# A chunked SSM scan by pairs of chunks, in a two-block transformer kernel

## Chip, cores and metric

The kernel runs on one core of one Trainium2 chip. The metric is the device time of one execution in microseconds (us); the time stated for a kernel is the median of its runs.

## What is computed

Two transformer blocks on 512 tokens of width 1024. The first mixes gated linear attention (GLA, four heads) with a grouped complex-diagonal state-space model (SSM) and ends in a feed-forward layer; the second has latent attention, a convolution and a mixture of experts. The change lies in the SSM of the first block. Its core in the reference:

```python
def step(carry, u_blk):
    h_re, h_im = carry
    bu_re = jnp.einsum('bcgh,gnh->bcgn', uf, bb_re)
    bu_im = jnp.einsum('bcgh,gnh->bcgn', uf, bb_im)
    acc_re, acc_im, x_re, x_im = lax.associative_scan(
        _complex_combine, (lam_b_re, lam_b_im, bu_re, bu_im), axis=1)
    s_re = x_re + acc_re * h_re[:, None] - acc_im * h_im[:, None]
    s_im = x_im + acc_re * h_im[:, None] + acc_im * h_re[:, None]
    y = jnp.einsum('bcgn,ghn->bcgh', s_re, cr) - jnp.einsum('bcgn,ghn->bcgh', s_im, ci)
    return (s_re[:, -1], s_im[:, -1]), y
```

That is x_t = L x_(t-1) + B u_t with a complex diagonal L, y_t = Re(C x_t) + D u_t, for 64 groups of 16 channels with 64 states each, and a gelu behind it. All is in float32; large products are made of three passes with operands split into a high and a low part.

## The kernel before

The 528 tokens (16 learned ones in front) are cut into 66 chunks of 8 (`NCH`). The SSM is computed in eighths of its groups (`ei`, 8 of them):

- `ssm_states` (L282): for each eighth a table G of the powers of L times B is formed, one half on DVE (L295 to L297), one on POOL (L299 to L301); PE transposes it (L307), ACT copies it out (L308), PE multiplies it with the inputs U (L314), and ACT writes each chunk's own contribution into the tile H (L317), which holds 66 chunks x real and imaginary x 32 columns.
- `ssm_scan` (L328): on POOL, for the chunks 1 to 64 one after the other, H[c] += L^8 H[c-1], as a 128x128 product (L334) and two 128x64 sums (L335, L336). `sct` is its buffer, in turn one of two.
- `ssm_out` (L407), a generator of steps: for each eighth `ssm_prep` (the tables CL on DVE, L352 to L354, a strip for short distances, stored to `k_dram`), `ssm_load` (U by POOL's queue, Tb by SP's and POOL's) and `ssm_main` (L380): ACT copies states from H into HS (L387), PE adds up L393 (Tb with U) and L396 (CL with HS), ACT makes the gelu ys (L399) and stores it to `gs_dram`.

Around it run the four heads of GLA: `gla_proj` (projections, PE's bulk work) and `gla_chain` (the recurrence). Generators are woven: `weave(main, fill)` takes a step of `fill` behind each step of `main`. The states and the scan are traced in the projections of heads 0 and 1; two steps of `outs` (the generator `ssm_out`) around head 2; and in head 3 `both(lagged(2), outs)` takes `outs` along from the fifth of six steps on (`LATE` = 4). What is left of it runs beside the last chain and `z_gate` (gate projections, eight units each for two gates, `zth`, stored to `gate_dram`). Then come `mix_gla` (L724; it loads o by L734 and splits it into ohi and olo), `load_gs` (L750; it loads `gs_dram` back and PE transposes it, L759) and `mix_ssm`.

Each engine works through its own queue in order. The order in a queue is made by a scheduler from the order of tracing and a simulated timeline; waits follow from the tiles that are read and written. Weights come by SP's queue (`raw`, L65), ACT casts the high part (`whi`, L73), DVE subtracts the low one (`wlo`, L74), one block ahead of its use (`Weights`); `raw` has two buffers.

Of the kernel before, what the change touches and what calls it, by code (L numbers as in the profile page):

```python
# [11 lines left out]
F32 = mybir.dt.float32  # L12
# [4 lines left out]
OP = mybir.AluOpType  # L17
# [6 lines left out]
NTOK = NMETA + SEQ  # L24
NCH = NTOK // 8
# [3 lines left out]
SPREAD = 14  # L29
BACK = 14  # L30
RATE = 2.0
LATE = 4
NS = 4
FIRST = 1
EARLY14 = 2
# [107 lines left out]
def sincos_exp(e, sp, mid, keep):  # L143

    nc, tc, A = e.nc, e.tc, e.A
    V = nc.vector
# [90 lines left out]
    V.tensor_scalar(lam[:, 0, 1], pw[:, 1, 8], -1.0, None, op0=OP.mult)  # L237
    V.tensor_copy(lam[:, 1, 0], pw[:, 1, 8])
    V.tensor_copy(lam[:, 1, 1], pw[:, 0, 8])
    zr, zi = T("x"), pw[:, 1, 1]  # L240
    V.tensor_scalar(zr, pw[:, 0, 1], -1.0, None, op0=OP.add)
    den, w = T("k"), T("p")
# [39 lines left out]
def ssm_states(e, sp):  # L282
# [3 lines left out]
    for ei in range(8):  # L286
# [23 lines left out]
        for ri in range(2):  # L310
            p = e.ps()
            for g2 in range(2):
                for q in range(4):
                    nc.tensor.matmul(p[64 * g2:64 * g2 + 64, q * NCH:(q + 1) * NCH],  # L314
                                     lhsT=GT[:, ri, q, 64 * g2:64 * g2 + 64], rhs=U[:, g2, q, :],
                                     start=True, stop=True)
            nc.scalar.copy(e.H[:, :, ri, q0:q0 + 4].rearrange("p c q -> p q c"),  # L317
                           p[:, :4 * NCH].rearrange("p (q c) -> p q c", q=4))


def load_u(e, sp, q0, bufs):
# [6 lines left out]
def ssm_scan(e, sp):  # L328
    nc = e.nc
    g = nc.gpsimd  # L330
    H = e.H
    for c in range(1, NCH - 1):
        t = e.sct[c % 2]
        g.tensor_mul(t, H[:, c - 1:c].to_broadcast([128, 2, 2, 32]), e.lam)  # L334
        g.tensor_add(H[:, c], H[:, c], t[:, :, 0])  # L335
        g.tensor_add(H[:, c], H[:, c], t[:, :, 1])  # L336


def ssm_prep(e, sp, ei):

    nc, A = e.nc, e.A
    V = nc.vector
    g0 = 8 * ei
    cr = sp.tile([128, 2, 8, 16], F32, name="craw", bufs=2)
    nc.gpsimd.dma_start(cr, A["ssm_c"][:, :, g0:g0 + 8, :])
    dsk = sp.tile([128, 2, 16], F32, name="dsk", bufs=2)
    nc.gpsimd.dma_start(dsk, A["d_diag"][:, ei])
    CL = sp.tile([128, 8, 9, 16], F32, name="CL", bufs=2)
    t = sp.tile([128, 8, 9, 16], F32, name="CLt", bufs=1)
    power = lambda i: e.pws[:, i, :, g0:g0 + 8].rearrange("p k g -> p g k")[:, :, :, None].to_broadcast([128, 8, 9, 16])  # L350
    coeff = lambda i: cr[:, i][:, :, None, :].to_broadcast([128, 8, 9, 16])
    V.tensor_mul(CL, power(0), coeff(0))  # L352
    V.tensor_mul(t, power(1), coeff(1))
    V.tensor_sub(CL, CL, t)  # L354
    p = e.ps()
    for s in range(2):
        for j in range(4):
            g = 4 * s + j
            nc.tensor.matmul(p[32 * j:32 * j + 32, s * 128:(s + 1) * 128],
                             lhsT=e.bs[:, g0 + g:g0 + g + 2].rearrange("p g h -> p (g h)"),  # L360
                             rhs=CL[:, g, 0:8].rearrange("p k h -> p (k h)"), start=True, stop=True)
    stt = sp.tile([128, 2, 128], F32, name="strip", bufs=1)
    nc.scalar.copy(stt.rearrange("p s n -> p (s n)"), p[:, :256])
    V.tensor_add(stt[:, :, 0:16], stt[:, :, 0:16], dsk)
    nc.gpsimd.dma_start(e.k_dram[g0:g0 + 8, :, 112:240].rearrange("(s j) h n -> (j h) s n", j=4), stt)
    return CL


def ssm_load(e, sp, ei):
    nc = e.nc  # L370
    U = load_u(e, sp, 4 * ei, 1)
    T = sp.tile([128, 8, 128], F32, name="Tb", bufs=1)
    kd = e.k_dram[8 * ei:8 * ei + 8, 0:16]
    for k in range(8):
        (nc.gpsimd if k % 2 else nc.sync).dma_start(T[16 * k:16 * k + 16],
# [4 lines left out]
def ssm_main(e, sp, ei, CL, U, T):  # L380
    nc = e.nc
    q0 = 4 * ei
    HS = sp.tile([128, 4, 2, 64], F32, name="HS", bufs=1)
    with behind(e, (e.k_last,)):
        for g2 in range(2):
            for ri in range(2):
# [337 lines left out]
def mix_gla(e, pool, ws):  # L724
# [3 lines left out]
    ohi = e.mb.tile([128, 8, 512], F32R, name="ohi", tag="u", bufs=3)  # L728
    olo = e.mb.tile([128, 8, 512], F32R, name="olo", tag="u", bufs=3)
    e.mixed = e.mb.tile([128, 8, 512], F32, name="mixed", tag="u", bufs=3)  # L730
    o = pool.tile([128, 8, 512], F32, name="o")
    for h in range(4):
        r = o[:, 2 * h:2 * h + 2]
        nc.sync.dma_start(r, e.o_dram[:, 2 * h:2 * h + 2])  # L734
        nc.scalar.copy(ohi[:, 2 * h:2 * h + 2], r)
        V.tensor_sub(olo[:, 2 * h:2 * h + 2], r, ohi[:, 2 * h:2 * h + 2].bitcast(F32))
# [1207 lines left out]
def block(ctx, tc, A, out, stop=None, dbg=None):  # L1944
# [78 lines left out]
    s_keep = ExitStack()  # L2023
    keep = s_keep.enter_context(P(name="ssmk", bufs=1, **R))
    e.H = keep.tile([128, NCH, 2, 32], F32, name="H")
    e.sct = [keep.tile([128, 2, 2, 32], F32, name=f"sct{i}") for i in range(2)]
    s1 = ExitStack()
    sp = s1.enter_context(P(name="ssm1", bufs=1, **R))
    wa, wgu = gate_weights(e, sp)
# [5 lines left out]
    s2 = ExitStack()  # L2035
    bpp = s2.enter_context(P(name="bp", bufs=1, **Lf))
    bp = bpp.tile([128, 4, NTOK], F32, name="bp")
    e.seg = bpp.tile([128, NTOK], F32, name="seg")
    nc.gpsimd.memset(e.seg, 1.0)
    for s0 in (0, 16, 144, 272, 400):  # L2040
        nc.gpsimd.memset(e.seg[:, s0:s0 + 1], 0.0)
    gp = s2.enter_context(P(name="gla", bufs=1, **Lf))
    e.Sb = [gp.tile([128, 4, 128], F32, name=f"Sb{i}") for i in range(2)]
    for t in e.Sb:
# [3 lines left out]
    for i in range(2):  # L2048
        last = nc.gpsimd.tensor_copy(e.xm[:, :, i * NMETA:(i + 1) * NMETA], e.xn[i][:, :, :NMETA])
    with P(name="gt", bufs=1, **R) as gtp:  # L2050
        kz = gtp.tile([128, 112], F32, name="kz")
        with tc.issue_after(last.ins):
            nc.gpsimd.memset(kz, 0.0)
# [27 lines left out]
                next(b, None)  # L2081
            yield

    def both(a, b):
        for i, _ in enumerate(a):
            if i >= LATE:
                next(b, None)
            yield
        for _ in b:
            yield  # L2090

    rest = scanned()
    weave(gla_proj(e, gp, 1, ws, parts[1]), twice(lagged(0), rest))
    for _ in rest:
# [5 lines left out]
    next(outs)  # L2100
    weave(gla_proj(e, gp, 2, ws, parts[2]), lagged(1))
    next(outs)
    weave(gla_proj(e, gp, 3, ws, parts[3]), both(lagged(2), outs))
    s_mb = ctx.enter_context(ExitStack())
    s4 = ExitStack()
    zz = s4.enter_context(P(name="zz", bufs=1, **R))
# [416 lines left out]
```

## Time and profile before

| | us |
|---|---|
| median of three runs | 1525.13 (1523.4 to 1525.76) |
| profiled execution, its own time | 1523.06 |
| its span, first to last instruction | 1521.2 |
| PE busy (matmul) | 1440.6 |
| PE weight load busy | 1198.0 |
| DVE busy | 882.6 |
| ACT busy | 655.8 |
| POOL busy | 510.7 |

PE is TensorE, DVE VectorE, ACT ScalarE, POOL GpSimd, SP SyncE; a q behind an engine's name is its queue of DMA issues. Busy times of the engines overlap. The granted clock is TensorE's share of full speed in a stretch: 1.00 is 2.4 GHz, 0.50 is 1.2 GHz.

### The profile page before, as it was taken

To read this page: it belongs to the slowest core of one execution; us is meant where nothing else is said; L and a number is where in the kernel's file an instruction comes from. 1 tells how busy PE (TensorE), PEld (TensorE's weight loads), DVE (VectorE), ACT (ScalarE), POOL (GpSimd) and SP (SyncE) were. 2 spreads that over 40 slices of the span, in tenths; PEclk is the share of its full clock that TensorE was granted. 3 is DMA by queue.
4 is the path that set the end of the run, shared out by engine and by line. 5 is a ranking of instruction groups with operands and counts; after the bars stand their busy time and mean duration, and the time that the engine had idled before them with its cause. 6 is when DMAs were issued, how large, how long until landed. Compare 5 with 4: busy or idle time off the path is not lost. (4 is left out here: it accounts for less than half of the span.)

```text
span 1521.2 us, 22633 instructions
## 1 busy us (share of the span) xinstructions
PE 1440.6 (95%) x8832; PEld 1198.0 (79%) x8832; DVE 882.6 (58%) x1539; ACT 655.8 (43%) x1081; POOL 510.7 (34%) x583
## 2 busy tenths in 40 slices
PE   7999999899999999999999999999999999978984
PEld 7989998677888899877787779987777877965542
DVE  6586644446245566645455454854798777544545
ACT  6464333545223343423313142547777673343323
POOL 0356888222001121412212121008877624012104
PEclk9999999999999999999999999999999999988997
DMA  5842232468553351655455444411222245868997
GB/s 211 189 93 99 86 93 101 107 170 253 169 209 111 127 206 36 214 180 176 143 194 180 153 165 139 151 59 55 96 75 72 90 153 215 347 246 313 413 407 166
DMA packets 73943, 253.42 MB, mean 167 GB/s; under 512 B 20912, under 2 KB 25792, under 8 KB 57188
## 3 DMA queue, kind: packets, MB, share of 16 engines
q1 hardware_dynamic: 38256, 180.18, 33.0%
q0 software_dynamic: 16192, 49.54, 11.7%
q10 hardware_dynamic: 19380, 22.17, 4.6%
q8 instruction: 72, 1.18, 0.3%
q14 instruction: 43, 0.35, 0.1%
HBM read 226.65 MB, written 32.17 MB: 170 GB/s over the span
## 5 line engine op out<-in xcount | busy, mean ns | idle before, releaser
L74 DVE TENSOR_TENSOR wlo<-raw,whi 128x2048 fp32r<-128x2048 f32 x73 | 177.7, 2434 | 125.5 <-ACT whi L73 125.5
L73 ACT CAST whi<-raw 128x2048 fp32r<-128x2048 f32 x76 | 145.2, 1910 | 195.3 <-PE ps L98 100.0
L1119 POOL TENSOR_TENSOR uc<-uc,u 128x512 f32<-128x512 f32 x77 | 114.7, 1490 | 92.5 <-ACT u L1116 86.0
L97 PE MATMUL ps<-xhi,whi 128*128 128x264 f32 (+1 forms) x352 | 119.0, 340 | 0.0
L98 PE MATMUL ps<-xlo,whi 128*128 128x264 f32 (+1 forms) x352 | 117.9, 335 | 0.3 <-DVE xlo L1932 0.3
L99 PE MATMUL ps<-xhi,wlo 128*128 128x264 f32 (+1 forms) x352 | 117.5, 334 | 0.0
L99 PE MATMUL ps<-hn,wlo 128*128 128x512 f32 (+1 forms) x256 | 97.7, 382 | 0.0
L98 PE MATMUL ps<-hn,whi 128*128 128x512 f32 (+1 forms) x256 | 97.6, 382 | 0.0
L97 PE MATMUL ps<-hn,whi 128*128 128x512 f32 (+1 forms) x256 | 97.5, 383 | 0.0
L866 DVE SCALAR_TENSOR_TENSOR aacc<-araw,ca,aacc 128x1024 f32<-128x1024 f32 x42 | 55.0, 1310 | 51.1 <-DMA araw<-in_ada_w_dram 50.8
L97 PE MATMUL ps<-whi,hh 128*128 128x512 f32 (+1 forms) x224 | 84.6, 378 | 0.0
L98 PE MATMUL ps<-wlo,hh 128*128 128x512 f32 (+1 forms) x224 | 84.1, 376 | 0.0
L99 PE MATMUL ps<-whi,hl 128*128 128x512 f32 (+1 forms) x224 | 83.9, 375 | 0.0
L905 POOL TENSOR_TENSOR fr<-fr 128x512 f32<-128x512 f32 x32 | 53.0, 1656 | 84.7 <-ACT fr L904 84.6
L862 POOL DMA_DIRECT2D araw<-in_ada_w_dram x48 | 26.3, 548 | 162.5 <-DVE aacc L866 94.5
L97 PE MATMUL ps<-whi,xhi 128*128 128x256 f32 x256 | 74.9, 292 | 0.0
L99 PE MATMUL ps<-whi,xlo 128*128 128x256 f32 x256 | 74.2, 290 | 0.0
L98 PE MATMUL ps<-wlo,xhi 128*128 128x256 f32 x256 | 73.5, 287 | 0.0
L97 PEld LDWEIGHTS ps<-xhi,whi 128*128 128x128 f32 x352 | 65.9, 188 | 8.9 <-issue 2.2
L99 PEld LDWEIGHTS ps<-xhi,wlo 128*128 128x128 f32 x352 | 66.3, 188 | 6.9
L98 PEld LDWEIGHTS ps<-xlo,whi 128*128 128x128 f32 x352 | 66.1, 188 | 6.8 <-DVE xlo L1932 0.5
L779 POOL TENSOR_TENSOR mixed<-mixed,mtb 128x512 f32<-128x512 f32 x8 | 12.5, 1559 | 152.7 <-DVE mtb L778 152.7
(673 smaller groups left out, 4162.4 us busy)
## 6 DMA issues: line engine op xcount, KB each, us to landing
raw<-in_w_ff_dram SPq DMA_DIRECT2D x28, 1024.0 KB
wg<-in_w_eg_dram SPq DMA_DIRECT2D x26, 1024.0 KB
araw<-in_ada_w_dram POOLq DMA_DIRECT2D x48, 512.0 KB
wd<-in_w_ed_dram SPq DMA_DIRECT2D x10, 1024.0 KB
raw<-in_w_glu_dram SPq DMA_DIRECT2D x8, 1024.0 KB
wse<-in_w_eg_dram SPq DMA_DIRECT2D x6, 1024.0 KB
y_dram<-wd SPq DMA_DIRECT2D x9, 512.0 KB
U<-u_dram POOLq DMA_DIRECT2D x16, 264.0 KB
```

The costliest lines, as they stand in the source:

```text
L73: nc.scalar.copy(hi[:, :n], raw[:, :n])
L74: sub.tensor_sub(lo[:, :n], raw[:, :n], hi[:, :n])
L97: nc.tensor.matmul(out, lhsT=ah, rhs=bh, start=(first and i == 0), stop=False)
L98: nc.tensor.matmul(out, lhsT=ah, rhs=bl, start=False, stop=False)
L99: nc.tensor.matmul(out, lhsT=al, rhs=bh, start=False, stop=(last and i == n - 1))
L779: nc.gpsimd.tensor_add(e.mixed[:, mm], e.mixed[:, mm], tb)
L862: nc.gpsimd.dma_start(raw, A["ada_w_2"][k * 128:(k + 1) * 128, i * DM:(i + 1) * DM])
L866: V.scalar_tensor_tensor(acc, raw, e.ca[:, k:k + 1], acc, op0=OP.mult, op1=OP.add)
L905: nc.gpsimd.tensor_mul(r, r, r)
L1119: nc.gpsimd.tensor_add(y, y, tmp)
```

## The change

Six edits go together.

1. The scan is made by pairs of chunks. `lam_step(e, 1, ..)`, six DVE instructions for an eighth (two products of 128x256 and four sums of 128x128), adds L^8 H[c-1] to all odd chunks of that eighth at once; it is traced one eighth behind the copies into H. `ssm_scan` then runs over the odd chunks only, 3 to 63, with the square of L^8 (`lam2`, six small DVE instructions in `sincos_exp`): 31 steps instead of 64. The even chunks are filled per eighth by `lam_step(e, 2, ..)`, ahead of the copies HS in `ssm_main`.
2. `sct` is one tile of 256 columns, used whole by `lam_step` and in halves by the scan.
3. CL is formed in two halves with half the buffer.
4. Tb gets two buffers.
5. The tile o in `mix_gla` becomes four tiles in three buffers; `seg`, the mask of the gates' scan, moves to another pool.
6. `both` is replaced by `second`, which takes a step of `outs` only behind the seventh step of `lagged(2)`; that generator has five, so none is taken in head 3.

```diff
@@ sincos_exp
+    lam2 = keep.tile([128, 2, 2, 32], F32, name="lam2", bufs=1)
+    V.tensor_mul(pt[:, 0], pw[:, 0, 8], pw[:, 0, 8])
+    V.tensor_mul(pt[:, 1], pw[:, 1, 8], pw[:, 1, 8])
+    V.tensor_sub(lam2[:, 0, 0], pt[:, 0], pt[:, 1])
+    V.tensor_copy(lam2[:, 1, 1], lam2[:, 0, 0])
+    V.scalar_tensor_tensor(lam2[:, 1, 0], pw[:, 0, 8], 2.0, pw[:, 1, 8], op0=OP.mult, op1=OP.mult)
+    V.tensor_scalar(lam2[:, 0, 1], lam2[:, 1, 0], -1.0, None, op0=OP.mult)
+    e.lam2 = lam2
@@ ssm_states, behind the copies into H
+        if ei:
+            lam_step(e, 1, q0 - 4)
+    lam_step(e, 1, 28)
+
+def lam_step(e, c0, q0):
+    V = e.nc.vector
+    q = slice(q0, q0 + 4)
+    t = e.sct.rearrange("p (c r q) -> p c r q", r=2, q=4)
+    for ro in range(2):
+        V.tensor_mul(t, e.H[:, c0 - 1:c0 + 63:2, :, q], e.lam[:, ro, :, q][:, None].to_broadcast([128, 32, 2, 4]))
+        for ri in range(2):
+            d = e.H[:, c0:c0 + 64:2, ro, q]
+            V.tensor_add(d, d, t[:, :, ri])
@@ ssm_scan
-    for c in range(1, NCH - 1):
-        t = e.sct[c % 2]
-        g.tensor_mul(t, H[:, c - 1:c].to_broadcast([128, 2, 2, 32]), e.lam)
+    for c in range(3, NCH - 2, 2):
+        t = e.sct[:, c % 4 // 2 * 128:c % 4 // 2 * 128 + 128].rearrange("p (o i q) -> p o i q", o=2, i=2)
+        g.tensor_mul(t, H[:, c - 2:c - 1].to_broadcast([128, 2, 2, 32]), e.lam2)
@@ ssm_prep
-    t = sp.tile([128, 8, 9, 16], F32, name="CLt", bufs=1)
-    V.tensor_mul(CL, power(0), coeff(0))
-    V.tensor_mul(t, power(1), coeff(1))
-    V.tensor_sub(CL, CL, t)
+    for g in (0, 4):
+        t = sp.tile([128, 4, 9, 16], F32, name="CLt", bufs=1)
+        V.tensor_mul(CL[:, g:g + 4], power(0, g), coeff(0, g))
+        V.tensor_mul(t, power(1, g), coeff(1, g))
+        V.tensor_sub(CL[:, g:g + 4], CL[:, g:g + 4], t)
@@ ssm_load
-    T = sp.tile([128, 8, 128], F32, name="Tb", bufs=1)
+    T = sp.tile([128, 8, 128], F32, name="Tb", bufs=2)
@@ ssm_main
+    lam_step(e, 2, q0)
@@ mix_gla
-    o = pool.tile([128, 8, 512], F32, name="o")
     for h in range(4):
-        r = o[:, 2 * h:2 * h + 2]
+        r = pool.tile([128, 2, 512], F32, name="o", bufs=3)
@@ block
-    e.sct = [keep.tile([128, 2, 2, 32], F32, name=f"sct{i}") for i in range(2)]
+    e.sct = keep.tile([128, 256], F32, name="sct")
-    e.seg = bpp.tile([128, NTOK], F32, name="seg")
+        e.seg = gtp.tile([128, NTOK], F32, name="seg")
-    def both(a, b):
-        for i, _ in enumerate(a):
-            if i >= LATE:
-                next(b, None)
-            yield
-        for _ in b:
-            yield
-    weave(gla_proj(e, gp, 3, ws, parts[3]), both(lagged(2), outs))
+    def second(a, b):
+        for i, _ in enumerate(a):
+            if i > 6:
+                next(b)
+            yield
+    weave(gla_proj(e, gp, 3, ws, parts[3]), second(lagged(2), outs))
```

## Rows read from the trace of the kernel before

**Rows 1.** Stretch 260 to 280: PE, PEld, DVE, ACT, POOL busy (count), clock, DMA, GB/s.

```profile
260.00:280.00 20.00, 13.16 (x88) 10.60 (x87) 6.01 (x9) 7.72 (x13) 10.69 (x26) 0.83 0.24 74
```

**Rows 2.** Waits between 264 and 280: total us, times, longest.

```profile
ACT HS L387 <- POOL H L336: 11.5, 1, 11.5
...
PE ps L396 <- ACT HS L387: 6.8, 2, 6.2
```

**Rows 3.** PE in order of time: start, us, instruction, [idle before <- releaser].

```profile
264.34 0.44 PE L393 MATMUL ps<-Tb,U 128*64 128x128 f32 x4
...
271.03 0.69 PE L396 MATMUL ps<-CL,HS 128*64 128x128 f32 x2 [6.25 <-ACT HS L387]
```

**Rows 4.** Stretch behind the idle time, columns as in rows 1.

```profile
271.00:276.50 5.50, 4.89 (x26) 3.33 (x28) 1.17 (x2) 3.63 (x6) 0.00 (x0) 0.51 0.02 3
```

**Rows 5.** Stretch of the later SSM outputs, columns as in rows 1.

```profile
280.00:400.00 120.00, 116.26 (x773) 91.18 (x773) 57.90 (x109) 58.56 (x89) 26.96 (x45) 1.00 0.69 194
```

**Rows 6.** POOL in order of time: the scan's first instruction and its last steps.

```profile
150.73 1.00 POOL L334 TENSOR_TENSOR sct<-H,lam 128x128 f32<-128x128 f32 x1
...
264.46 0.46 POOL L334 TENSOR_TENSOR sct<-H,lam 128x128 f32<-128x128 f32 x1
...
268.45 0.45 POOL L334 TENSOR_TENSOR sct<-H,lam 128x128 f32<-128x128 f32 x1
...
269.38 0.32 POOL L336 TENSOR_TENSOR H<-H,sct 128x64 f32<-128x64 f32 x1
```

**Rows 7.** DVE and POOL in order of time: single instructions.

```profile
43.82 0.28 DVE L225 TENSOR_TENSOR pw<-pw 128x128 f32<-128x128 f32 x1
...
105.53 1.51 DVE L633 TENSOR_TENSOR E<-E,k 128x256 f32<-128x256 f32 x1
...
244.24 2.35 DVE L74 TENSOR_TENSOR wlo<-raw,whi 128x2048 fp32r<-128x2048 f32 x1 [7.48 <-ACT whi L73]
...
244.52 2.39 POOL L334 TENSOR_TENSOR sct<-H,lam 128x128 f32<-128x128 f32 x1
...
250.80 0.43 DVE L633 TENSOR_TENSOR E<-E,k 128x256 f32<-128x256 f32 x1
```

**Rows 8.** Stretch of the states, columns as in rows 1.

```profile
98.00:150.00 52.00, 49.25 (x540) 45.73 (x539) 41.07 (x37) 26.68 (x44) 33.49 (x27) 1.00 0.29 96
```

**Rows 9.** That stretch: PE's wait, a DVE product, POOL's product by line.

```profile
PE ps L307 <- DVE G L297: 1.5, 3, 0.8
...
119.49 0.69 DVE L295 TENSOR_TENSOR G<-pw,bb 128x512 f32<-128x512 f32 x1 [0.48 <-PE ps L307]
...
L299 POOL TENSOR_TENSOR G<-pw,bb 128x512 f32<-128x512 f32 x6 | 10.2, 1696 | 1.5 <-PE ps L307 1.2
```

**Rows 10.** SP, ACT and PE in order of time, around outputs and o.

```profile
346.45 0.43 SPq L65 DMA_DIRECT2D raw<-in_w_zs_dram  x1
...
348.61 1.05 ACT L735 CAST ohi<-o 128x1024 fp32r<-128x1024 f32 x1 [4.17 <-DMA o<-o_dram]
...
379.02 0.64 ACT L387 COPY HS<-H 64x256 f32<-64x256 f32 x1
...
390.02 0.39 PE L396 MATMUL ps<-CL,HS 128*64 128x128 f32 x4
```

**Rows 11.** The end of the outputs: engines in order, DMA stretches, L759's instructions.

```profile
391.77 0.60 ACT L399 ACTIVATE ys<-ps 128x512 f32<-128x512 f32 x1 [1.31 <-PE ps L396]
...
396.50:397.00 0.50, 0.50 (x4) 0.41 (x3) 0.00 (x0) 0.00 (x0) 0.00 (x0) 1.00 0.00 0
...
399.26 2.29 DVE L74 TENSOR_TENSOR wlo<-raw,whi 128x2048 fp32r<-128x2048 f32 x1 [10.95 <-ACT whi L73]
...
401.58 0.32 SPq L65 DMA_DIRECT2D raw<-gs_dram  x1
...
404.00:404.50 0.50, 0.50 (x3) 0.40 (x3) 0.00 (x0) 0.00 (x0) 0.00 (x0) 1.00 0.23 90
...
L759 PE MATMUL ps<-ident,raw x32: 270/272/273, 413.9 to 455.7; 128*128 128x128 f32 x32
```

More of the change, by code (lines that the diff above doesn't have):

```diff
@@ L31 @@
 RATE = 2.0
-LATE = 4
 NS = 4
@@ L348, in ssm_prep @@
     CL = sp.tile([128, 8, 9, 16], F32, name="CL", bufs=2)
-    t = sp.tile([128, 8, 9, 16], F32, name="CLt", bufs=1)
-    power = lambda i: e.pws[:, i, :, g0:g0 + 8].rearrange("p k g -> p g k")[:, :, :, None].to_broadcast([128, 8, 9, 16])
-    coeff = lambda i: cr[:, i][:, :, None, :].to_broadcast([128, 8, 9, 16])
-    V.tensor_mul(CL, power(0), coeff(0))
-    V.tensor_mul(t, power(1), coeff(1))
-    V.tensor_sub(CL, CL, t)
+    power = lambda i, g: e.pws[:, i, :, g0 + g:g0 + g + 4].rearrange("p k g -> p g k")[:, :, :, None].to_broadcast([128, 4, 9, 16])
+    coeff = lambda i, g: cr[:, i, g:g + 4][:, :, None, :].to_broadcast([128, 4, 9, 16])
+    for g in (0, 4):
[3 more added lines that the diff above has]
+        V.tensor_sub(CL[:, g:g + 4], CL[:, g:g + 4], t)
     p = e.ps()
@@ L2037, in block @@
     bp = bpp.tile([128, 4, NTOK], F32, name="bp")
-    e.seg = bpp.tile([128, NTOK], F32, name="seg")
-    nc.gpsimd.memset(e.seg, 1.0)
-    for s0 in (0, 16, 144, 272, 400):
-        nc.gpsimd.memset(e.seg[:, s0:s0 + 1], 0.0)
     gp = s2.enter_context(P(name="gla", bufs=1, **Lf))
@@ L2050, in block @@
     with P(name="gt", bufs=1, **R) as gtp:
+        e.seg = gtp.tile([128, NTOK], F32, name="seg")
+        nc.gpsimd.memset(e.seg, 1.0)
+        for s0 in (0, 16, 144, 272, 400):
+            nc.gpsimd.memset(e.seg[:, s0:s0 + 1], 0.0)
         kz = gtp.tile([128, 112], F32, name="kz")
```

## Prediction

> **What bounds the kernel now.** I read the busy times first, then the table of stretches, then the waits, then the engines' lists around the one hole. PE is busy 1440.6 of 1521.2 us, so a change outside PE pays only where PE waits or runs at its low clock. Around the scan one stretch of 20 us stands out: from 260 to 280 us PE works only 13.16 us and its mean granted clock is 0.83 [rows 1]. The waits say why: ACT's copies HS (L387) waited 11.5 us for the last instruction of the scan on POOL (L336), and PE's L396 waited for HS, 6.8 us in two waits [rows 2]. In PE's own list the first four matmuls of the first SSM output (L393) start at 264.34, and L396 starts at 271.03 after 6.25 us of nothing [rows 3]; the other wait is the rest of the 6.8, 0.6 us. The granted clock tells the rest: after the hole PE gets 0.51, the lower level of 1.2 GHz, from 271.0 to 276.5, half of the 2.4 GHz that it has at 1.00 [rows 4]. So the scan ends too late for the place that the first SSM output has in PE's order. Elsewhere between 280 and 400 us PE is idle for only 3.7 of 120 us [rows 5].
>
> **What the change takes away: the hole.** The scan runs from 150.73 until 269.70 us: 64 steps, 1.86 us each on the average, 1.33 us where nothing disturbs one (268.45 - 264.46 is three steps) [rows 6]. The new one has 31 steps of the same three instructions, so 31 x 1.86 = 58 us, and ends near 153 + 58 = 211 us. Besides, the first output is traced later: with lagged(2) yielding five times, `i > 6` never comes, so the two steps of `outs` that lay in the last head are run by the loop behind it. The copies HS then stand at least one unit of z_gate and one step of chain 3 behind their old place. Either edit alone removes the wait: moved by two units of about 5.5 us (below), L396 would come at 264.8 + 11 = 276 us, and the old scan with the two copies for the first half would be through at 269.7 + 1.3 = 271. What is saved: 6.8 us of waiting, and half of the 4.89 us that PE worked at 0.51, 2.4 us [rows 2, 4]. Sum 9.2 us. Next late after it would be the small waits of the stretch from 280 to 400, 3.7 us in all [rows 5]; I leave them, with 3.7 us more gain as the lower bound: the second buffer of Tb may take some of them.
>
> **What it adds ahead of the scan.** lam_step(e, 1, ..) puts six DVE instructions behind each eighth: two of 128x256 and four of 128x128. The nearest rows: a 128x256 product took 0.43 us alone and 1.51 us beside POOL work, a 128x128 product 0.28 us [rows 7]. So one lam_step is 2 x 0.43 + 4 x 0.28 = 2.0 us undisturbed. I take the strides at nothing: a product of L295, which reads two broadcast views, took 0.69 us for 512 columns [rows 9], no more for an element than L633. Six of the eight lie between 98 and 150 us: 12 us more for DVE, which is busy 41.07 of 52 us there, so 10.9 are free [rows 8]. PE is idle for only 2.75 us there, but it does wait for DVE's G three times, 1.5 us in all [rows 8, 9]: G comes just in time. The free time lies after G, while DVE waits for PE to take G away (0.48 us ahead of that L295, released by L307 [rows 9]), and lam_step falls into it, traced an eighth back so that its H is long there. I take 3 us of new PE waiting, one half us for each of six. Bounds: nothing, and about 8 us. The last two lie past 150, where they only move the start of the scan by some 2 us, which no longer matters.
>
> Here a rule of the chip speaks against the change. The trace: beside a 2.35 us DVE instruction of L74 a scan product on POOL took 2.39 us where it takes 0.46 [rows 6, 7], and DVE's 128x256 product took 1.51 instead of 0.43 [rows 7]. The Trainium skill ("SBUF — State Buffer", section "SBUF: two separate sides") calls the port pair that VectorE and GpSimd share an exclusive lock: a VectorE instruction with two inputs in SBUF and a GpSimd one that reads SBUF exclude each other for a whole instruction. By that rule the six new instructions wait in line with G's three POOL products, and the trace agrees in these rows; what this would cost is the first rival.
>
> **What else it adds or moves.** Edits whose cost I put at nothing, with their cover:
> - lam_step(e, 2, ..) in ssm_main: 2.0 us of DVE for each of eight outputs, 16 us where DVE is busy 57.9 of 120 us [rows 5]. It stands ahead of HS on ACT, a new wait: behind it queue ACT's next casts and tanhs, and PE's L396 waits for HS. Cover: the copies HS for the last output begin at 379.02 and L396 uses them at 390.02 [rows 10], 11 us less 2.6 for four copies. Without cover, 2 us each.
> - lam2: six instructions of 128x32, under 6 x 0.28 = 1.7 us, long before the scan. seg's memset only moves. CL by halves: six instructions for three, some 0.1 us more each, in DVE's free half.
> - o with three buffers: its fourth load on SP waits for the first cast, which begins at 348.61; behind it SP holds the w_zs load, now issued at 346.45 [rows 10]. It could come some 4 us later; the weights are split one block ahead of PE, about 11 us. Cover enough.
> - The later outputs. Every load, store and matmul of each main, load and prep goes with them: on POOL past nothing, since the scan is over sooner, on SP behind one more load of weights. The end matters: the last output's ys starts at 391.77, as its matmuls end, and the transposes of gs_dram (L759) begin at 413.9, with three units of z_gate and one of mix_gla between them, so 22.1 / 4 = 5.5 us for a unit [rows 11]. With two units fewer there are 11.1 us for ys, its store and the load. In the rows gs_dram's load was issued at 401.58, when wlo (399.26 + 2.29) gave its raw buffer back; the DMA engines were idle from 396.5 on, 4.7 us behind the matmuls, and the load itself was moving data until 404.5, some 3 us [rows 11]. 4.7 + 1 to be told + 3 = 8.7 of 11.1 us. No new stall; bounds 0 and 3 us, I take 0.
>
> **The sum.** -9.2 (hole and low clock) + 3 (DVE ahead of the scan) = -6.2 us. The profiled execution took 1523.06 us, 1.9 of it outside its span of 1521.2; it is 2.1 us below the median of the three timed runs, and I hang the difference on the median: 1525.1 - 6.2 = 1518.9.
>
> **The rivals.**
> 1. *The shared port turns lam_step into a bottleneck* (slower). Between 98 and 150 us POOL runs three products of G for an eighth (L299 six times, 1.7 us on the average [rows 9]), and each can hold up one new DVE instruction by 1.51 - 0.43 = 1.1 us. At three holds for a lam_step it costs 2.0 + 3.3 = 5.3 us, six of them 32 us, against 10.9 us free: 21 us too much. Some 6 of it, an estimate, can push back products of CL and of the gated-attention chain that PE does not need soon; 15 would reach PE. Time: 1525 - 9.2 + 15 = 1531. It decides for slower from 9.2 + 3 us of new waiting on, a lam_step of about 5 us. For it: G already makes PE wait. Against it: POOL's and DVE's idle gaps do not all coincide, and the holds are partly paid already.
> 2. *Half of that* : lam_step at about 3.8 us, six of them 23 us, 12 over the free time, 6 through to PE: 1525 - 9.2 + 6 = 1522 to 1525.
> 3. *One wait for another*: HS(0) waits for its new DVE work instead of POOL, which stands behind casts and sr, and PE idles as long as before. It needs a delay of over the 8 us of cover; time 1525. Little speaks for it.
> 4. *The shorter scan does nothing*: moving the outputs alone clears the hole, and the DVE work buys nothing. The change's time is then that of the forecast, but the move alone would give 1525.1 - 9.2 = 1516.
>
> **How the numbers follow.** Forecast (with 4, which gives the same time): 1513 to 1522, chance 0.62. Rival 2: 1522 to 1526, 0.16. Rival 3: 1525, 0.09. Rival 1: 1527 to 1533, 0.13. Within 0.2%, what a measurement of this kernel can tell from no change, is 1522.1 to 1528.2: 0.16 + 0.09 = 0.25. Faster 0.62, slower 0.13. The range takes the forecast with its lower bound (1518.9 - 3.7 - 3 = 1512) and reaches over rivals 2 and 3: 1512.5 to 1527.
>
> **What would show it.** Right: no idle PE over 1 us and a clock of 1.00 from 255 to 300 us; POOL's scan over near 211 us; 98 to 150 us stretched by about 3 us, with waits of L307 for G as their name; lam_step instructions of 0.2 to 0.5 us with some near 1.5. Wrong: PE waiting for HS again, with DVE named; a hole ahead of L759; or over 9 us of new idle time between 98 and 150 us. The scheduler also orders each engine anew, which I can't see: a moved matmul group elsewhere would spoil a us or two either way.

## Result and the profile after

The changed kernel takes 1534.94 us (median of seven runs, 1529.29 to 1541.49), the kernel before, run beside it, 1525.13: a ratio of 1.0062 with an interval of 1.0045 to 1.0079, some 9.5 us slower. The forecast was 6.2 us faster, 1518.9 in a range of 1512.5 to 1527; the measured time lies above that range. The profiled execution took 1535.01 us, its span is 1533.2.

The hole that the change was to close is closed. Two large new ones have taken its place, both ahead of it in time. Stretches of the changed kernel, columns as in rows 1 (stretch, then busy time and count of PE, PEld, DVE, ACT, POOL, then granted clock, DMA share, GB/s):

```profile
98.00:150.00 52.00, 42.76 (x439) 39.99 (x438) 50.94 (x67) 23.66 (x39) 32.09 (x25) 0.95 0.30 98
...
260.00:280.00 20.00, 20.00 (x150) 18.01 (x149) 9.60 (x12) 10.70 (x20) 0.00 (x0) 1.00 0.35 116
280.00:400.00 120.00, 115.50 (x735) 88.67 (x733) 63.47 (x130) 54.47 (x86) 24.47 (x40) 0.97 0.62 171
```

From 260 to 280 us PE now works all of 20.00 us at 1.00, where it worked 13.16 at 0.83 [rows 1]. From 98 to 150 it works 42.76 of 52 us where it worked 49.25 [rows 8], and DVE, which had 10.9 us free there, has 1.1.

PE in order of time: start, us, instruction, [idle before <- releaser].

```profile
147.29 1.08 PE L314 MATMUL ps<-ident,G 128*128 128x128 f32 x4 [5.97 <-DVE G L304]
...
235.31 1.22 PE L699 MATMUL ps<-v,kT 128*128 128x256 f32 x2 [4.28 <-DVE St L700]
...
297.04 0.44 PE L721 MATMUL ps<-ident,St 128*128 128x128 f32 x2 [1.86 <-DVE St L716]
...
363.22 0.65 PE L382 MATMUL ps<-CL,bs 128*32 128x128 f32 x8 [2.53 <-DVE CL L377]
```

(L314 and L304 are L307 and L297 of before; L699 is the state update of a GLA head, L721 the transposes of its output, L382 the matmuls with CL. Line numbers shift by a few in the runs below.) All four name DVE. Behind each the clock drops to its lower level:

```profile
144.00:152.00 8.00, 4.71 (x25) 4.74 (x26) 7.36 (x14) 1.17 (x2) 2.88 (x3) 0.57 0.10 30
232.00:240.00 8.00, 4.69 (x18) 4.32 (x19) 7.68 (x21) 0.47 (x2) 0.00 (x0) 0.58 0.40 131
298.00:302.00 4.00, 4.00 (x36) 3.49 (x36) 1.27 (x3) 0.79 (x3) 0.00 (x0) 0.57 0.08 32
362.00:366.00 4.00, 2.78 (x13) 2.04 (x14) 3.35 (x5) 1.07 (x2) 1.40 (x3) 0.63 1.03 349
```

Busy time times what is missing to a clock of 1.00 is what it cost, an estimate: 4.71 x 0.43 = 2.0, 2.0, 1.7 and 1.0, together 6.7 us, against 2.4 us of before behind its one hole. The idle gaps of PE of 0.4 us and more between 10 and 500 us add up to 20.5 us, against 12.2 before. 8.3 + 4.3 = 12.6 us; and the transposes of gs_dram begin at 426.6, 12.7 us later than the 413.9 of before [rows 11]. From there to the end the distance stays, within a microsecond. So the loss lies ahead of 426 us, and is idle time and low clock of PE. 2.9 of the 8.3 us are a wait of PE at 79 us, ahead of the states; in the profiles of the runs below, with the same code up to there, it is between 0 and 1.8 us, so I don't count it to the change; 9.7 us are left, about the measured loss. Both profiles also have low clock near 80 us, which is in none of these sums: by the same reckoning it cost 2.0 us here (78.5 to 83.5, 4.32 busy at 0.53) and 3.5 before (74.5 to 82, 7.50 at 0.54).

What DVE did in front of the first hole (start, us, instruction):

```profile
137.92 0.41 DVE L337 TENSOR_TENSOR sct<-H,lam 128x256 f32<-128x256 f32 x1
138.25 1.59 DVE L303 TENSOR_TENSOR Gt<-pw,bb 128x512 f32<-128x512 f32 x1
139.77 2.84 DVE L340 TENSOR_TENSOR H<-H,sct 128x128 f32<-128x128 f32 x2
142.64 1.92 DVE L337 TENSOR_TENSOR sct<-H,lam 128x256 f32<-128x256 f32 x1
144.59 0.62 DVE L340 TENSOR_TENSOR H<-H,sct 128x128 f32<-128x128 f32 x2
145.31 0.42 DVE L337 TENSOR_TENSOR sct<-H,lam 128x256 f32<-128x256 f32 x1
145.65 0.68 DVE L302 TENSOR_TENSOR G<-pw,bb 128x512 f32<-128x512 f32 x1
...
146.46 0.68 DVE L304 TENSOR_TENSOR G<-G,Gt 128x512 f32<-128x512 f32 x1
```

POOL in the same stretch:

```profile
140.00 1.12 POOL L306 TENSOR_TENSOR G<-pw,bb 128x512 f32<-128x512 f32 x1
141.19 1.26 POOL L308 TENSOR_TENSOR G<-G,Gt 128x512 f32<-128x512 f32 x1
...
143.15 1.12 POOL L307 TENSOR_TENSOR Gt<-pw,bb 128x512 f32<-128x512 f32 x1
```

The next eighth's G (L302, L304) stands behind a lam_step that should have taken 2 us. Two of its sums took 2.84 us and one product 1.92, while POOL ran its own products of G (from 140.00 to 144.3). Right behind, with POOL quiet, the other two sums took 0.62 and the next product 0.42. PE has nothing in the meantime and waits 5.97 us.

What DVE did in front of the second hole:

```profile
220.15 0.29 DVE L661 TENSOR_TENSOR d<-bp 128x16 f32<-128x16 f32 x1
227.50 0.42 DVE L337 TENSOR_TENSOR sct<-H,lam 128x256 f32<-128x256 f32 x1 [7.07 <-POOL H L358]
...
230.39 2.28 DVE L73 TENSOR_TENSOR wlo<-raw,whi 128x2048 fp32r<-128x2048 f32 x1
...
234.18 0.48 DVE L700 SCALAR_TENSOR_TENSOR St<-St,dc,ps 128x256 f32<-128x256 f32 x1
```

The first lam_step(e, 2, ..) reads what the scan writes last (L358), and waits 7.07 us for it at the head of DVE's queue. Behind it come the rest of this step, most of the next eighth's, a wlo, two products of the head's own, and the St (L700) that PE's L699 wants. The wait that ACT had for the scan [rows 2] is now DVE's, and DVE hands it on to PE.

### The profile page after: what moved, and what is told of

It is laid out like the page before. It is cut to its first block, busy times and chain, and to the rows that moved or that the text cites. A ratio compares the mean times of both kernels' runs of the same rounds, so it can differ in the third digit from the quotient of the medians.

```text
span 1533.2 us, 22643 instructions
## 1 busy us (share of the span) xinstructions
PE 1446.6 (94%) x8832; PEld 1201.2 (78%) x8832; DVE 914.1 (60%) x1665; ACT 653.2 (43%) x1079; POOL 463.5 (30%) x484
## 5 line engine op out<-in xcount | busy, mean ns | idle before, releaser
L96 PEld LDWEIGHTS ps<-hn,whi 128*128 128x128 f32 x256 | 48.0, 188 | 12.6 <-ACT whi L72 1.7
```

The source lines that it names most:

```text
L96: nc.tensor.matmul(out, lhsT=ah, rhs=bh, start=(first and i == 0), stop=False)
```

## The experiments

They were made against these explanations. **Order**: an instruction that waits, or is long, stands in an in-order queue ahead of one that PE needs; where it stands decides (theory 1 below, F where letters are used). **Time**: the added DVE work costs PE wherever it stands (theory 2, G). **Hold-up**: two-input instructions of DVE and instructions of POOL hold each other up, so the added work is longer among POOL's products (theory 3, C). Times are medians; a ratio is to the kernel before, run beside it on the same chip (its medians were 1522.65 to 1525.13). In the edits, `with behind(e, (x,))` makes the scheduler put what is traced inside it behind the instruction x in its engine's queue.

### The outputs moved, and nothing else

```diff
 kernel before
-    weave(gla_proj(e, gp, 3, ws, parts[3]), both(lagged(2), outs))
+    weave(gla_proj(e, gp, 3, ws, parts[3]), lagged(2))
```

> The kernel before with the sixth edit alone: the SSM outputs are not taken along in the last head, the scan stays on POOL chunk by chunk with 64 steps. Theory A (the loss comes from the new DVE work, the move alone clears the hole): the 6.2 us of idle PE at L396 and the low clock behind it are gone, the stretch from 98 to 150 us is as before, time 1514 to 1519 us, a ratio of 0.993 to 0.996. Rival B (the move itself does the harm, through later holes such as the 1.9 us at 297 and the 2.5 us at 363 of the changed kernel): idle PE of 4 us or more between 280 and 430 us, time 1523 to 1530. Rival C (a scan of 64 steps is still too late for the new place): PE waits for HS again, time near 1525.

Measured: 1522.54 us, ratio 0.9996 (0.9985 to 1.0007). ACT in order of time in that run:

```profile
269.90 2.50 ACT L387 COPY HS<-H 64x256 f32<-64x256 f32 x4 [11.57 <-POOL H L336]
272.43 0.60 ACT L597 ACTIVATE th<-ps 128x512 f32<-128x512 f32 x1
272.92 0.38 ACT L686 ACTIVATE kT<-ps 128x256 f32<-128x256 f32 x1
```

PE in the same stretch:

```profile
273.56 1.22 PE L684 MATMUL ps<-v,Sb 128*128 128x256 f32 x2 [4.47 <-ACT kT L686]
```

PE no longer needs HS at that time, but the copies HS are still at the same place in ACT's queue, wait 11.57 us as before, and the Square (L686) whose kT PE's L684 does need stands behind them. The hole has changed its name.

### The first copies HS behind the Squares

```diff
 the kernel above, in ssm_main; e.sq_last is the last Square of head 2
-    with behind(e, (e.k_last,)):
+    with behind(e, (e.k_last if ei else e.sq_last,)):
```

> The kernel before with the outputs moved (the run e1_move_only), and in it only the first output's copies HS stand behind the last Square of head 2 in ACT's queue; all others keep their place. Theory 1 (order in ACT's queue: the Square that PE needs through kT stands behind an HS that waits for the scan): the hole of 4.47 us at 273 and the low clock of 272 to 279 are gone, with no new hole at 313 to 325 as in the run where every output's copies were moved; 1515 to 1518. Rival (the hole is not the queue's, or the moved copies make PE's first output late): a hole of 3 us or more between 270 and 290 by another name, 1521 to 1524.

Measured: 1514.86 us, ratio 0.9942 (0.9914 to 0.9969). PE works 19.95 us of the 20 from 260 to 280 at a clock of 1.00:

```profile
260.00:280.00 20.00, 19.95 (x129) 18.03 (x128) 9.52 (x18) 7.32 (x16) 9.78 (x22) 1.00 0.20 60
```

So the move is worth what was forecast for it, 9 us, once the queue of ACT is put in order too. (The odd and even steps play no part in it: its scan is that of before.)

### All copies HS behind the Squares

```diff
 the kernel of the first experiment
-    with behind(e, (e.k_last,)):
+    with behind(e, (e.sq_last,)):
```

> The kernel before with the sixth edit alone, and the copies HS queued on ACT behind the last square of the head whose chain is then under way. In the run with the sixth edit alone PE no longer waited for HS but for a square that stood behind HS in ACT's queue, 4.5 us. Theory F: with the copies behind the squares that hole goes and its low clock with it, with a scan of 64 steps as before; time 1514 to 1518, a ratio of 0.994 to 0.997. Rival H (another instruction takes the place at the head of ACT's queue or the hole has another cause): idle PE of 3 us or more between 262 and 285 us, time 1521 to 1525.

Measured: 1527.57 us, ratio 1.003 (1.002 to 1.0039). The hole at 273 is gone, but this edit put the copies of every output behind the Squares of its own head, and later ones came too late: PE waits 1.76 us for HS at 317, and 2.94 at 325 for CL, whose DVE product had waited for that output's matmuls. Waits of 2.28 us for a Square at 313 and 3.09 for CL at 359 came up as well; I can't show that the copies made these two. The expectation of 1514 to 1518 was missed. A place in a queue cuts both ways.

### The pairs, with the outputs at their old place

```diff
 kernel after
-    weave(gla_proj(e, gp, 3, ws, parts[3]), second(lagged(2), outs))
+    weave(gla_proj(e, gp, 3, ws, parts[3]), both(lagged(2), outs))
```

> The changed kernel with the outputs back in the last head, two steps of them from its fifth step on. Theory A: the holes of the new DVE work stay (about 6 us at the transposes of G near 147 us, about 4 us behind the end of the scan), and HS does not wait for POOL since the scan is over by about 228 us; the move gives nothing once the scan is short, so the time is that of the changed kernel, 1531 to 1537 us. Rival B (the move does harm): 1525 to 1530 us.

Measured: 1528.98 us, ratio 1.004 (1.0025 to 1.0054). The holes of 4.87 us at 145 and 4.21 us at 233 are there, PE does not wait for HS. The short scan alone removes that wait; and moving the outputs costs 1.0062 - 1.004 = 0.2%, 3 us, instead of bringing something. The two intervals overlap, so this pair alone does not settle it; a second pair follows below.

### The changed kernel without the odd, without the even step

```diff
 kernel after, first run (the odd chunks lack their even neighbour's share)
-        if ei:
-            lam_step(e, 1, q0 - 4)
-    lam_step(e, 1, 28)
 kernel after, second run (the even chunks lack theirs)
-    lam_step(e, 2, q0)
```

> The changed kernel without the combining steps for the odd chunks ahead of the scan, so those chunks lack the share of their even neighbour; all else stays. Theory A (they fill DVE's queue between the tables G): the 6 us at the transposes near 147 us and most of the 3 us between 100 and 122 us go, the scan starts near 155 instead of 165 us, the first projection products behind the states come some 8 us earlier, time 1523 to 1528. Rival D (shared port alone, POOL holding DVE up whoever is added): the same holes stay by over half.

> The changed kernel without the filling of the even chunks, so they lack the share of their odd neighbour; all else stays. Theory A (its first one stands in DVE's queue and waits there for the end of the scan, with the head's own work queued behind it): DVE's 7 us of idle time ahead of 227 us and PE's 4.3 us at the recurrence's L699 go, with the low clock behind them, time 1526 to 1530 us. Rival E (DVE was late there for other reasons, its plain load): PE waits at L699 as before, time 1532 to 1537.

Measured: 1517.82 us without the odd step, ratio 0.9969 (0.9952 to 0.9987), and 1526.01 without the even one, 1.0015 (1.0003 to 1.0027). The first is 5 us under the least that was expected of it. Against 1.0062 the odd step costs 0.93%, 14 us, the even one 0.47%, 7 us. Without the odd step there is no hole near 145, and the one near 235 is down to 1.56 us; without the even step the first stays at 5.97 and the second is gone.

### The even step later in DVE's queue, or on POOL

```diff
 kernel after, first run; e.v_last is the first product sr of the last head
-    lam_step(e, 2, q0)
+    with behind(e, (e.v_last,)):
+        lam_step(e, 2, q0)
 kernel after, second run; the last argument is the engine
-    lam_step(e, 2, q0)
+    lam_step(e, 2, q0, nc.gpsimd)
```

> The changed kernel with every filling step of the even chunks queued on DVE behind the first product sr of the last head (the 128x512 product of th), so that none of them can stand ahead of that head's work and wait for the scan. Nothing is left out. Theory F (a waiting instruction at the head of an in-order queue is what costs, not the DVE time): DVE's 7 us of idle time and PE's 4.3 us near 235 us go as they did without the filling, time 1525 to 1529 us against some 1532 to 1535 of the changed kernel. Rival G (DVE time as such): sixteen us of it have to be done somewhere, time 1531 to 1536.

> The changed kernel, but the even chunks' lam_step(e, 2, ..) runs on POOL, which has little to do once the scan has ended; the odd chunks' stay on DVE. Theory 1 (order in DVE's queue): DVE no longer waits 7 us for the scan's end at 220 to 227, PE's 4.28 us wait for St at 235 and the low clock behind it are gone, and no wait comes up near 290; the 5.97 us wait near 147 stays. Time 1525 to 1527, that of the kernel without the even step (1526.0). Theory 3 (the two engines hold each other up): POOL's six instructions take 1 us and more each beside DVE's two-input ones, DVE's slow down too, HS comes late, and the time stays above 1529.

Measured: 1530.28 us, ratio 1.0047 (1.0031 to 1.0064), and 1530.85, 1.0035 (1.002 to 1.0051). Both clear the hole at 235, as theory 1 says, and both give part of it back; the first time can't be told from that of the changed kernel (1.0045 to 1.0079). In the first the steps fall among the small DVE instructions that make the factor for the head's St:

```profile
291.10 0.69 PE L724 MATMUL ps<-ident,St 128*128 128x128 f32 x2 [4.44 <-DVE St L719]
```

In the second PE waits 3.13 us for CL at 357, where the changed kernel has 2.53 and the one without the even step 1.29. That kernel's 1526 was expected of it and missed by 5 us (by the ratios 3, with intervals that overlap); where the rest of these went I can't show.

### The odd steps traced together, behind the last eighth

```diff
 kernel after
-        if ei:
-            lam_step(e, 1, q0 - 4)
-    lam_step(e, 1, 28)
+    for q0 in range(0, 32, 4):
+        lam_step(e, 1, q0)
```

> The changed kernel with the eight combining steps of the odd chunks traced together behind the last eighth of the states. Nothing is left out, the DVE instructions are the same in number and size. Theory F: G is just in time again, the idle PE of 5 to 6 us at the transposes near 146 us goes, the first recurrence products come some 7 us earlier, time 1524 to 1529. Rival C (the shared port, held by POOL's products): the scheduler or the port stretches G as before, time 1531 to 1536. Against both: the block of 16 us delays the scan and with it the filling, which already blocks DVE; then the hole near 235 us grows by what is saved, time near 1532.

Measured: 1530.78 us, ratio 1.0043 (1.0026 to 1.006). The scheduler puts the steps among the G's again, as soon as their H is there; the hole at 144 is 5.97 us as before. The order of tracing does not settle the order of the queue. The next run forces it.

### The odd steps forced behind the last G

```diff
 kernel after
-        V.tensor_sub(G[:, 0], G[:, 0], t[0])
+        last = V.tensor_sub(G[:, 0], G[:, 0], t[0])
...
-        if ei:
-            lam_step(e, 1, q0 - 4)
-    lam_step(e, 1, 28)
+    with behind(e, (last,)):
+        for q0 in range(0, 32, 4):
+            lam_step(e, 1, q0)
```

> The changed kernel, but all eight lam_step(e, 1, ..) stand on DVE behind the last table product of G, so none stands between two G's. Theory 1 (order in DVE's queue: a G that PE needs stands behind a lam_step): the 5.97 us wait of PE for G near 147 and the three small ones of 103 to 122 are gone, and the low clock of 144 to 152 with them, some 10 us of PE; but the scan starts some 16 us later (near 180 instead of 165) and ends near 242, and DVE's Sb and St work behind the block comes later, so a new wait for DVE of 3 to 6 us may come between 150 and 240. Time 1526 to 1531 if it does, 1522 if it doesn't. Theory 2 (DVE's time counts, wherever it stands): no gain, 1533 to 1535 as the changed kernel. Theory 3 (POOL and DVE hold each other up): most of it gone too, as POOL is idle behind its last G; the new instructions take 0.28 to 0.5 us each, 16 us for eight steps.

Measured: 1519.5 us, ratio 0.9965 (0.995 to 0.9981), faster than before, and better than expected of any theory. PE's waits for DVE's G from 96 to 160 us are those of the kernel before [rows 9], to the tenth:

```profile
PE ps L314 <- DVE G L304: 1.5, 3, 0.8
```

The scan starts at 185.2 us and ends at 242, 15 us later than in the changed kernel, and DVE waits 3.8 us for it; nothing that PE needs stands behind, and there is no idle gap of 0.4 us in PE between 150 and 280. So neither the 16 us of odd work nor the even steps behind the scan make PE wait at such a place. That refutes theory 2. Whether the place matters for its order or for POOL's products beside it, this run doesn't tell.

### One input instead of two, at the same place

```diff
 kernel after; one_input goes over as many elements of H, writes to sct, and not to H
 (the odd chunks lack their even neighbour's share)
-            lam_step(e, 1, q0 - 4)
-    lam_step(e, 1, 28)
+            one_input(e, 1, q0 - 4)
+    one_input(e, 1, 28)
...
+def one_input(e, c0, q0):
+    for ro in range(2):
+        V.reduce_sum(e.sct[:, :64].rearrange("p (c r) -> p c r", r=2), e.H[:, c0 - 1:c0 + 63:2, :, q], axis=X)
+        for ri in range(2):
+            V.reduce_sum(e.sct[:, 64 + 32 * ri:96 + 32 * ri], e.H[:, c0:c0 + 64:2, ri, q], axis=X)
```

> The changed kernel, but each lam_step(e, 1, ..) is replaced by six sums over H of as many input elements with one operand in place of two, at the same place between the G's (the odd chunks then lack their even neighbour's share). Undisturbed they should take about as long, 2.0 to 2.4 us for an eighth. Theory 3 (two-input instructions of DVE and POOL's hold each other up): they are not stretched to the 4.1 us that a lam_step takes among the G's in the changed kernel, and PE's wait for G near 147 shrinks from 5.97 to under 2 us, with no low clock there; 1521 to 1526. Theory 1 with theory 2 (DVE's plain time in front of G): the stretch or the hole stays, 4 to 6 us near 147, and the time is 1530 or more.

Measured: 1520.08 us, ratio 0.9979 (0.9966 to 0.9991). DVE's groups from 98 to 150 us (count | busy us, mean ns | idle before), in the changed kernel:

```profile
L340 DVE TENSOR_TENSOR H<-H,sct 128x128 f32<-128x128 f32 x20 | 13.9, 694 | 0.4
...
L337 DVE TENSOR_TENSOR sct<-H,lam 128x256 f32<-128x256 f32 x10 | 6.2, 622 | 0.2
```

The same groups in this run, where sums of one operand stand in their place:

```profile
L351 DVE TENSOR_REDUCE sct<-H 128x32 f32<-128x128 f32 x26 | 7.0, 274 | 3.4 <-ACT H L324 3.3
...
L349 DVE TENSOR_REDUCE sct<-H 128x64 f32<-128x256 f32 x13 | 5.3, 406 | 0.0
```

Five steps of the changed kernel took 13.9 + 6.2 = 20.1 us, 4.0 each. The means mix two kinds: one by one, 8 of the 20 sums took 1.09 to 1.79 us and two of the 10 products 0.98 and 1.92, all ten beside a product of POOL; the other twenty took 0.28 to 0.29 and 0.41 to 0.42. Six and a half of the one-input kind took 12.3 us, 1.9 each, among the same products of POOL. Behind the last G, in the run before this one, the real ones take 292 and 422 ns (the same stretch and columns):

```profile
L340 DVE TENSOR_TENSOR H<-H,sct 128x128 f32<-128x128 f32 x8 | 2.3, 292 | 0.3
...
L337 DVE TENSOR_TENSOR sct<-H,lam 128x256 f32<-128x256 f32 x4 | 1.7, 422 | 0.1
```

PE's wait for G near 147 shrinks with it from 5.97 to 1.78 us, and no low clock follows:

```profile
140.92 1.07 PE L314 MATMUL ps<-ident,G 128*128 128x128 f32 x8 [1.78 <-DVE G L304]
```

So it is the hold-up: the same place costs little when the added instructions read one operand. The sums of this run also write less, 32 or 64 columns in place of 128 or 256. Lines of the changed kernel tell these two apart:

```profile
125.40 1.30 POOL L308 TENSOR_TENSOR G<-G,Gt 128x512 f32<-128x512 f32 x1
...
125.41 0.68 DVE L622 SCALAR_TENSOR_TENSOR sr<-th,ps 128x512 f32<-128x512 f32 x1
126.00 0.98 DVE L337 TENSOR_TENSOR sct<-H,lam 128x256 f32<-128x256 f32 x1
```

sr writes 512 columns and has two operands, but ps lies in PSUM, the memory that matmuls write to, so only one of them lies in SBUF, the memory of the other tiles here. It ran wholly beside POOL's L308 in 0.68 us, and no sr of this kernel took over 0.69. The product behind it, with half the columns and both operands in SBUF, took 0.98 where it takes 0.42. So what is held up is an instruction with two operands in SBUF, however much it writes. Order comes in because the stretched instructions stand in front of G. The time of the run says a little less than the trace, since its sums don't write H: its scan starts at 154.3 instead of 165.2, which takes some of the wait at 220 to 227 away too.

### Both steps on POOL

```diff
 kernel after; last is POOL's last instruction of G
+    with behind(e, (last,)):
+        for q0 in range(0, 32, 4):
+            lam_step(e, 1, q0, e.nc.gpsimd)
...
+    lam_step(e, 2, q0, nc.gpsimd)
```

> The changed kernel, but all lam_steps run on POOL: the eight odd ones behind POOL's last G, the even ones behind the scan. DVE has no new work but lam2 and CL's halves. Theory 1 (order in DVE's queue) and theory 2 (DVE's time) both expect the waits at 147 and at 235 gone and some 1515 to 1519, a little under the kernel without the odd step (1517.8); the scan starts behind some 25 us of odd steps, near 178, and ends near 240, still ahead of the first HS (264 of before or later). Theory 3 (the two engines hold each other up for whole instructions): POOL's 48 instructions between 153 and 180 slow down DVE's two-input ones as they did before, and the time is 1525 or more.

Measured: 1526.3 us, ratio 1.0014 (0.9999 to 1.0029); 7 us and more above what theories 1 and 2 expected. The hole near 147 is gone, and PE waits for DVE's St at two other places:

```profile
181.70 1.22 PE L698 MATMUL ps<-v,kT 128*128 128x256 f32 x2 [3.14 <-DVE St L699]
...
289.29 0.44 PE L720 MATMUL ps<-ident,St 128*128 128x128 f32 x2 [4.11 <-DVE St L715]
```

DVE was held up without having more to do: among POOL's steps its two-input product of 128x512 (E with q, L649) took 1.22 us at 177; in the run with the steps behind G, with POOL quiet, its like took 0.69 at 172:

```profile
177.32 1.22 DVE L649 TENSOR_TENSOR E<-E,q 128x512 f32<-128x512 f32 x1
...
171.91 0.69 DVE L650 TENSOR_TENSOR E<-E,q 128x512 f32<-128x512 f32 x1
```

The hold-up goes both ways.

### The layout edits alone

```diff
 kernel before; CL also in halves, as in the change
-    T = sp.tile([128, 8, 128], F32, name="Tb", bufs=1)
+    T = sp.tile([128, 8, 128], F32, name="Tb", bufs=2)
...
-        r = o[:, 2 * h:2 * h + 2]
+        r = pool.tile([128, 2, 512], F32, name="o", bufs=3)
...
-    e.seg = bpp.tile([128, NTOK], F32, name="seg")
+        e.seg = gtp.tile([128, NTOK], F32, name="seg")
```

> The kernel before with the edits of layout alone: CL in halves, two buffers of Tb, o in four tiles with three buffers, seg in another pool. Scan, outputs and their place are as before. All theories: these are hidden, time within 2 us of the kernel before, ratio 0.9985 to 1.0015, with the hole at HS near 265 us as before. If instead one of them costs, it shows as a new wait of PE between 300 and 430 us or a later start of the gates near 75 us, and the time is 1526 or more.

Measured: 1523.54 us, ratio 1.0006 (0.9993 to 1.0019), with the HS hole in its place (8.00 us at 274).

### Odd steps behind the last G, outputs at the old place

```diff
 the kernel with the odd steps forced behind the last G
-    weave(gla_proj(e, gp, 3, ws, parts[3]), second(lagged(2), outs))
+    weave(gla_proj(e, gp, 3, ws, parts[3]), both(lagged(2), outs))
```

> The run with the odd steps behind the tables (1519.5), and the SSM outputs left at the old place, from the fifth step of head 3's chain on. There the first HS comes at about 264 to 270, the scan ends near 242 and the even step runs behind it, so nothing waits. If the move costs 4 to 6 us of its own, as between the changed kernel (1534.9) and the one with the old place (1529.0): 1514 to 1516, and it ties with the run of the first copies behind the Squares (1514.9). If the move's cost came only from the holes that the odd and even steps made: 1518 to 1521.

Measured: 1514.44 us, ratio 0.9942 (0.9923 to 0.9962): with the first copies behind the Squares the fastest here, and by a way of its own. Its stretches:

```profile
98.00:150.00 52.00, 49.89 (x547) 46.36 (x546) 44.65 (x53) 25.79 (x42) 33.14 (x27) 1.00 0.29 96
...
260.00:280.00 20.00, 19.97 (x152) 16.87 (x150) 15.08 (x38) 11.46 (x20) 1.46 (x2) 1.00 0.29 86
280.00:400.00 120.00, 117.70 (x741) 89.97 (x742) 54.92 (x107) 55.02 (x80) 25.93 (x43) 1.00 0.69 197
```

The only idle gaps of PE over 0.6 us between 98 and 500 are these two, and no stretch of 2 us between 82 and 500 us has a clock below 0.99:

```profile
281.04 0.41 PE L722 MATMUL ps<-ident,St 128*128 128x128 f32 x2 [1.06 <-DVE St L717]
...
351.80 0.44 PE L418 MATMUL ps<-Tb,U 128*64 128x128 f32 x4 [1.26 <-DMA Tb<-k_dram]
```

Against the same kernel with the outputs moved (0.9965) the move costs 0.23%, as it did in the other pair (0.22%). In each pair the intervals overlap; that both agree is what speaks for it. In the run with the outputs moved PE's gaps are 2.21 us for St at 282, 1.44 for CL at 345 and 1.29 for Tb at 353.

## Why the prediction was wrong

The step that failed is the price of lam_step(e, 1, ..): it was put at its undisturbed 2.0 us and at 3 us of new PE waiting in all, where the runs show 4.0 us a step among POOL's products and some 14 us of the time. A second term, lam_step(e, 2, ..), stood at nothing and cost some 7.

The hold-up was named, as rival 1, and given 0.13. That rival has the mechanism of the first hole, but neither the low clock behind it nor the second hole, where DVE waits for the scan; the measured 1534.9 lies above its 1527 to 1533 too. Its 15 us for PE are near the 14 in part by luck: it priced a step at 5.3 us, three holds of 1.1; measured are ten holds in five steps, about 1.0 us each. Of the 14, PE's waits for G make 8.9 - 1.5 = 7.4 and the low clock behind the longest 2.0; the rest, about, is the wait near 235, 4.28 us with 2.0 of low clock, which without the odd step is 1.56 us with none.

The steps of the prediction in order:

- **The hole, -9.2 us.** Right in size. With the pairs and the old place PE waits for nothing there, and the kernel with nothing else wrong is 0.58% (8.8 us) faster than before.
- **"Either edit alone removes the wait"**, and with it rival 4 (1516 by the move alone). Half wrong. The short scan alone does it. The move alone gave 1522.5: I moved PE's L396 in the sum, and left out that the copies HS keep their place in ACT's queue, with a Square behind them that PE needs. With that mended as well it gave 1514.9.
- **lam_step(e, 1, ..), +3 us.** This is the term that failed; by the runs it is some 14. The undisturbed length, 2.0 us, was right (2 x 422 + 4 x 292 ns = 2.0), and so was the guess for it if nothing disturbs: with one-input sums of 1.9 us at the same place, PE works 46.86 of the 52 us, 2.4 less than before (1.6 of it a wait for ACT's GT at 100). What failed is the choice of the value. The rows showed a 128x256 product of 1.51 us beside POOL and 0.43 alone [rows 7], and POOL was busy 33.49 of the 52 us [rows 8], yet I took 0.43 and put the other value into a rival. It took 4.0 us a step, close to the 3.8 of rival 2 and over what DVE had free (five steps, not six, lay there: 20.1 us, free 10.9). One-input sums beside the same POOL products took 274 and 406 ns, the two-input instructions 694 and 622 on the mean. The row of 1.51 us should have carried the sum. The Trainium skill's rule ("SBUF — State Buffer", section "SBUF: two separate sides": a two-input VectorE instruction and a GpSimd one that reads SBUF shut each other out) agrees with these numbers.
- **"It falls into DVE's free time after G."** Wrong: it stood in front of the next G (L337 and L340 from 139.77 to 145.2, G at 145.65). That a queue has 10.9 us free does not say that they lie ahead of the instruction that is late. The bound of 8 us of new waiting was nearly met (8.9 us in four waits of PE for G against 1.5 in three), but the wait of 6 us was also followed by the low clock, 2.0 us, and the sum had counted the low clock only where it went away, not where it could come.
- **lam_step(e, 2, ..), at nothing.** 7 us. The cover that I named (11 us) was that of the last output, far behind the scan. The first output's step stands at the scan's end, where the wait is the scan's, and its place in DVE's queue is ahead of wlo and St. I had asked who waits behind it on ACT, and not who waits behind it on DVE.
- **The scan's end, near 211.** It came at 227.5: started at 165.2 instead of 153, since it waits for the last of the odd sums, which the hold-ups had made late, and 31 steps took 2.0 us each, not 1.86. That made the wait of the even step long.
- **The move, 0 with a bound of 3 us.** About 3.4 us (0.22 and 0.23%). No hole stands ahead of the transposes of gs_dram (L759 of before), where I looked; the 1 us "to be told" in that cover is measured by no run here. The loss shows in small waits for St, CL and Tb between 280 and 355.
- **Layout edits at nothing.** Right (1.0006).
- **Rival 3**, HS waiting for its new DVE work, did not come: PE does not wait for HS at all.

Put together, from ratios: the hole -9, the odd steps among the G's +14, the even step +7 (part of it caused by the odd ones), the move +3. That is +15 against 9.5 measured, so the parts overlap by some 5 us. Putting the odd steps behind the last G gains 0.97% in one go and leaves PE no wait at the even step either.

What stays open: why the even step on POOL does not reach the time of the kernel without it, and which of the small waits between 280 and 360 the move makes directly and which through other places in the queues.

## What to carry to other kernels

Price work that is added to an engine at what the same kind of instruction took beside the other engines of that stretch, not at what it takes alone; on DVE, count the operands that lie in SBUF, and look at what POOL does meanwhile. Free time of an in-order queue counts only ahead of the instruction that is due next: put added work behind the last producer that the bound engine waits for, and a step that waits for a late result behind all that is due before that result (this second half is argued from the wait at 235 us; the run that did it alone gained too little to tell). When a consumer is moved, the copy that feeds it is moved in the queue of its own engine too, or its wait is handed on to whatever stands behind.

## What the runs showed of the hardware

- A 128x128 sum of two operands on DVE took 292 ns on the mean with POOL quiet, 694 ns among POOL's 128x512 products; a sum of one operand with as many columns took 274 ns among the same products. The 694 is made of 12 sums at 0.28 to 0.29 us and 8 at 1.09 to 1.79 that ran beside a POOL product. I had not expected the difference to be this clean.
- POOL's side: a 128x256 product of lam_step took 0.73 us with DVE quiet (184 to 190 us, both steps on POOL), 910 ns on the mean of all 16 of the odd steps.
- In the changed kernel, gaps in PE of 1.86 us (297 us) and 2.53 us (363 us) were followed by 4 us at a clock of 0.57 and 0.63. One of 1.78 us at 141 in the one-input run was not, nor one of 2.21 at 282 in the run with the odd steps behind G; what tells them apart the runs don't show.
